# A two-layer encoder trunk: half of one tile's low-part products moved ahead of transposes, one product parted, and the mixer's products held to their written order

## The chip, the cores and the metric

One core of a Trainium2 chip runs the whole kernel. The metric is the device time of one execution in microseconds; three runs of the kernel before gave a median of 1097.06 us (1096.51 to 1097.66).

## What is computed

The reference is a two-layer encoder over 256 tokens of width 1024. Each layer has three sub-layers: a half-step SwiGLU feed-forward, a token mixer, and a second feed-forward. Each sub-layer starts with an RMS norm whose result is scaled and shifted by vectors that come from a conditioning input.

```python
for l in range(DEPTH):                      # 2
    n1 = modulate(rms_norm(h, norm_g[l, 0]), sh1, sc1)
    h = h + 0.5 * g1 * swiglu(n1, ffn_wg[l, 0], ffn_wu[l, 0], ffn_wd[l, 0])
    n2 = modulate(rms_norm(h, norm_g[l, 1]), sh2, sc2)
    y = token_mixing(n2, ...)    # 8-head grouped-query + 4-head differential attention, sigmoid gates, w_o
    h = h + g2 * y
    n3 = modulate(rms_norm(h, norm_g[l, 2]), sh3, sc3)
    h = h + 0.5 * g3 * swiglu(n3, ffn_wg[l, 1], ffn_wu[l, 1], ffn_wd[l, 1])
return rms_norm(h, final_g)
```

All data is float32. D_FF is 2816, so a feed-forward has 11 slices of 256 hidden columns.

## The kernel before

**Products.** TensorE (PE) works on float32r operands. Each operand is split into a high part and a low part (`whi`, `wlo` for a weight, `nh`, `nl` for the normed tokens), and a product is three matmuls: high by high, low by high, high by low (`mm3`, L85). Weights stream in from memory as units of 1 MB through four `raw` buffers. `pump` (L317) turns half a unit into `whi` (a copy on ScalarE, ACT, L328) and `wlo` (a subtraction on VectorE, DVE, L330). The same stream also carries conditioning units, which DVE reduces (L245) or adds into a gate row `gacc` (L276). `done` gives back the slots of a used half and pumps more. `load_next` issues the next load on SP's queue as soon as a unit has been used up.

**Boundaries.** Tokens stand in two tiles of 128. `boundary` (L444) ends a sub-layer and starts the norm of the next one. For tile 1 that is the residual (L441, L442), the sum of squares on ACT (L369), `rstd` on GpSimd (POOL, L124), the scaling `xs` on DVE (L394), eight transposes on PE (`transposes`, L403), then `nh` on ACT (`mod_hi`, L414) and `nl` on DVE (`mod_lo`, L426 and L429). `BT` (L35) holds for each kind of sub-layer how many halves of `mod_lo` of tile 0 are written early and how many `pump` calls stand before and after the end of tile 1's norm. The next sub-layer starts with the products of tile 0: `tok_hi` (L493) makes the 16 matmuls of 512 columns that need only `nh`, `tok_lo` (L505) the 8 that need `nl`. In a feed-forward these fill `gu`; in the mixer they fill `qa`, and the key and value projection `kv` follows. There are five boundaries: into the mixer of each layer, out of it, and from layer 0 to layer 1.

**Order.** The program is written as one list of instructions. A planner at compile time orders each engine's queue: of what its own timing says is ready it takes what is written first. The written order is therefore a priority, not the order of execution. `follow` (L90) adds an edge that forces one instruction behind another on the same engine. At run time each engine works through its queue in the planned order.

**The mixer around the change.** Its written order after the projections (L1026 to L1042) is: the query rows of tile 0 are transposed (`to_T` of `qr`), the key rows of tile 0 (`to_T` of `kr`), 48 products of the `qd` projection (`proj_T`, bank name `pt`), key rows of tile 1 are finished (`post_kv`), query rows and key rows of tile 1 are transposed, 48 more `qd` products, scores of tile 0 (`a_scores(0, 0)`, 12 matmuls), 48 `kd` products, scores of tile 1 (`a_scores(0, 1)`), 48 `kd` products, and the transposes `a_T(0, 0)` of the softmax rows of both tiles (bank name `pt` too, L875). Then come the 24 matmuls of the `vd` projection of tile 0, `a_T(0, 1)`, `a_scores(1, 0)` and the `vd` projection of tile 1. From there on, gate products (`gt`) stand between the attention steps.

A key row tile `kr` comes from this chain: squares on ACT, a reduction `hms` on DVE (L762), two small POOL steps (L763, L124), and a scaling on DVE (L825). A softmax row tile `p` comes from a maximum on DVE (`nmx`, L844), exponentials on ACT (L852), and a scaling (L864 on ACT for one key head, L866 on DVE for the other).

Of the kernel before, what the change touches and what calls it, by code (L numbers as in the profile page):

```python
# [34 lines left out]
BT = [(1, 1, 1), (1, 3, 1), (1, 1, 1)]  # L35
# [7 lines left out]
def trunk(tc, a):  # L43
    nc = tc.nc
    with (
# [38 lines left out]

        def mm3(out, Lh, Ll, Rh, Rl, start, stop):  # L85
            nc.tensor.matmul(out, Lh, Rh, start=start, stop=False, skip_group_check=True)  # L86
            nc.tensor.matmul(out, Ll, Rh, start=False, stop=False, skip_group_check=True)  # L87
            nc.tensor.matmul(out, Lh, Rl, start=False, stop=stop, skip_group_check=True)  # L88
# [26 lines left out]
        for hf in range(2):  # L115
            x = slice(hf * 512, (hf + 1) * 512)
            bank = gen("cb")
            cmm = nc.tensor.matmul(bank, ones[0:1, :], crow[hf], start=True, stop=True)
            cact = nc.scalar.activation(cb[:, x], bank, AF.Silu)
# [169 lines left out]
        def gate_bcast(l, s):  # L289
# [5 lines left out]
            for hf in range(2):  # L295
# [5 lines left out]
                nc.tensor.matmul(bank, onesr, gh, start=True, stop=False, skip_group_check=True)  # L301
                nc.tensor.matmul(bank, onesr, gl, start=False, stop=True, skip_group_check=True)
# [57 lines left out]
        class Norm:  # L360
# [37 lines left out]
            def transposes(self):  # L398
                self.banks = []
                for hf in range(2):  # L400
                    bank = gen("nt")
                    for i in range(4):
                        nc.tensor.transpose(bank[:, i * P:(i + 1) * P], self.xs[hf][:, i * P:(i + 1) * P], ident)  # L403
# [89 lines left out]
        def tok_hi(bank, ncol, unit_of, nT, t):  # L493
# [4 lines left out]
            for k in range(NK):  # L498
# [3 lines left out]
                nc.tensor.matmul(bank, nh[:, k, tok], wh[:, x], start=k == 0, stop=False, skip_group_check=True)  # L502
                nc.tensor.matmul(bank, nh[:, k, tok], wl[:, x], start=False, stop=False, skip_group_check=True)
# [45 lines left out]
        def first_T(hts):  # L549

            tb = gen("tb")
            for t in range(2):
                for c in range(2):
                    nc.tensor.transpose(tb[:, c * 256 + t * P:c * 256 + (t + 1) * P], hts[t][:, c * P:(c + 1) * P], ident)
# [6 lines left out]
        def ffn(i, nT, norm1, first, nT_next):  # L561
# [6 lines left out]
            def down_mm(idx, t, hf, last, y=slice(0, 512), part=False):  # L568
# [4 lines left out]
                for c in range(2):  # L573
                    x = slice(c * 512 + y.start, c * 512 + y.stop)
                    if part and c == 1:

                        for L, R in ((hh, wh), (hl, wh)):
                            nc.tensor.matmul(acc[t][hf], L[:, c, tok], R[:, x], start=False, stop=False, skip_group_check=True)
                        for z in (slice(0, PART), slice(PART, 512)):
                            nc.tensor.matmul(acc[t][hf][:, z], hh[:, c, tok], wl[:, 512 + z.start:512 + z.stop], start=False,  # L580
# [19 lines left out]
            else:  # L600
# [7 lines left out]
                tok_hi(banks[0], 512, uo, nT, 0)  # L608
                norm1.transposes()
# [107 lines left out]
        def mixer(i, nT, norm1, consts, nT_next):  # L717
# [65 lines left out]
            def to_T(src, dst, t, n):  # L783

                bank = gen("tt")
                for i in range(n):
                    nc.tensor.transpose(bank[:, i * P:(i + 1) * P], src[:, i * P:(i + 1) * P], ident)
# [44 lines left out]
            def a_scores(jj, t):  # L832
# [3 lines left out]
                for i in range(2):  # L836
                    for x, y in ((0, 0), (1, 0), (0, 1)):
                        for v in range(2):
                            pr = slice(v * 64, (v + 1) * 64)
                            nc.tensor.matmul(banks[v][:, i * 256:(i + 1) * 256], st["qaT"][x][pr, 2 * jj + i, tok], kaT[y][pr, 0, :],  # L840
# [29 lines left out]
            def a_T(jj, i):  # L870
                for v in range(2):
                    bank = gen("pt")
                    for t in range(2):
                        for c in range(2):
                            nc.tensor.transpose(bank[:, c * 256 + t * P:c * 256 + (t + 1) * P],  # L875
# [5 lines left out]
            def a_pv(jj):  # L881
                ot = gen("ot")

                for i in range(2):
                    for c in range(2):
                        for v in range(2):
                            nc.tensor.matmul(ot[v * 64:(v + 1) * 64, i * 256:(i + 1) * 256], va[:, c, v * 64:(v + 1) * 64],
# [12 lines left out]
            def b_scores(pair, t):  # L900
# [3 lines left out]
                for m in range(2):  # L904
                    ch = m * 2 + pair
                    for x, y in ((0, 0), (1, 0), (0, 1)):
                        for e in range(2):
                            pr = slice(e * 64, (e + 1) * 64)
                            nc.tensor.matmul(scs[e][:, m * 256:(m + 1) * 256], st["qdT"][x][pr, ch, tok], st["kdT"][y][pr, ch, :],
# [26 lines left out]
            def b_T(hd):  # L936
                bank = gen("wt")
                for t in range(2):
                    for c in range(2):
                        nc.tensor.transpose(bank[:, c * 256 + t * P:c * 256 + (t + 1) * P], xs[hd, t][0][:, c * P:(c + 1) * P], ident)  # L940
# [465 lines left out]
```

## Time and profile before

| what | value |
|---|---|
| median of three runs | 1097.06 us |
| the profiled execution, its own time | 1097.68 us |
| its span, first to last instruction | 1095.9 us |
| PE busy | 1082.9 us, 99% of the span |
| DVE busy | 864.9 us, 79% |
| ACT busy | 593.1 us, 54% |
| DMA | 271.12 MB, mean 247 GB/s |

Rows of a timeline give start and duration in us, the engine, the line, the operation, what it writes from what, its shape and a count; in brackets stands idle time ahead of it and what ended that. Durations of matmuls hold a modelled end, so spacing is read from one start to the next.

### The profile page before, as it was taken

How to read it: one execution, taken by the hardware profiler on the slowest of the kernel's cores; microseconds unless marked ns; L12 is line 12 of the kernel's file. 1: busy time of each engine (PE TensorE's matmuls, PEld its weight loads, DVE VectorE, ACT ScalarE, POOL GpSimd, SP SyncE). 2: the span in 40 equal slices, each digit the busy share in tenths (PEclk: the TensorE clock that was granted, in tenths of full speed). 3: DMA queues.
4: the chain of work that ended last, by engine and by line, in shares of the span. 5: the costliest groups of instructions: out<-in, count | busy, mean ns of one | idle time of the engine just before them, and what ended most of it. 6: DMA issues, size and time to landing. Idle time of an engine off the chain costs nothing.

```text
span 1095.9 us, 19235 instructions
## 1 busy us (share of the span) xinstructions
PE 1082.9 (99%) x7796; PEld 998.8 (91%) x7796; DVE 864.9 (79%) x1388; ACT 593.1 (54%) x916; POOL 44.5 (4%) x52
## 2 busy tenths in 40 slices
PE   8999999999999999999999999999999999999997
PEld 6989999898999899999989999989889998999996
DVE  5998986899978798886589886569988779766543
ACT  5564483558664554535455545435776547444432
POOL 1000000220010000000000000004000000000000
PEclk9999999999999999999999999999999999999999
DMA  8998996368745299997449987543865454876501
GB/s 315 380 368 336 380 335 219 120 263 332 264 172 193 86 376 357 347 377 266 150 152 357 365 288 285 202 165 126 297 236 189 157 190 183 315 267 229 197 19 39
DMA packets 44889, 271.12 MB, mean 247 GB/s; under 512 B 5880, under 2 KB 6648, under 8 KB 14848
## 3 DMA queue, kind: packets, MB, share of 16 engines
q1 hardware_dynamic: 42340, 267.93, 66.1%
q10 hardware_dynamic: 2460, 1.96, 0.6%
q8 instruction: 61, 1.00, 0.3%
q14 instruction: 28, 0.23, 0.1%
HBM read 268.82 MB, written 1.05 MB: 246 GB/s over the span
## 4 chain that ended last, share of the span: by engine, by line
PE 94%; DVE 3%; ACT 1%; issue 1%; POOL 0%; POOLq 0%
PE dn L87 6%; PE dn L88 6%; PE dn L86 6%; PE u L86 6%; PE g L86 6%; PE u L87 6%; PE g L88 6%; PE g L87 6%; PE u L88 6%; PE gt L86 3%; PE gt L88 3%; PE gt L87 3%; PE g L1199 2%; PE u L1199 2%; PE yb L88 1%; PE yb L87 1%
## 5 line engine op out<-in xcount | busy, mean ns | idle before, releaser
L330 DVE TENSOR_TENSOR wlo<-raw,whi 128x1024 fp32r<-128x1024 f32 x364 | 436.9, 1220 | 133.7 <-PE u L87 44.6
L328 ACT CAST whi<-raw 128x1024 fp32r<-128x1024 f32 x364 | 374.0, 1052 | 226.4 <-PE u L88 83.7
L86 PE MATMUL u<-nh,whi 128*128 128x256 f32 x592 | 164.0, 277 | 0.0
L86 PE MATMUL g<-nh,whi 128*128 128x256 f32 x592 | 164.0, 277 | 0.0
L87 PE MATMUL u<-nh,wlo 128*128 128x256 f32 x592 | 163.7, 277 | 0.0
L88 PE MATMUL g<-nl,whi 128*128 128x256 f32 x592 | 163.7, 277 | 0.0
L87 PE MATMUL g<-nh,wlo 128*128 128x256 f32 x592 | 163.7, 277 | 0.0
L88 PE MATMUL u<-nl,whi 128*128 128x256 f32 x592 | 163.6, 276 | 0.0
L86 PE MATMUL dn<-whi,hh 128*128 128x512 f32 (+1 forms) x326 | 126.0, 387 | 0.0
L87 PE MATMUL dn<-whi,hl 128*128 128x512 f32 (+1 forms) x326 | 125.9, 386 | 0.0
L88 PE MATMUL dn<-wlo,hh 128*128 128x512 f32 (+1 forms) x326 | 125.8, 386 | 0.0
L86 PEld LDWEIGHTS g<-nh,whi 128*128 128x128 f32 x592 | 111.2, 188 | 0.3
L87 PEld LDWEIGHTS g<-nh,wlo 128*128 128x128 f32 x592 | 111.2, 188 | 0.2
L86 PEld LDWEIGHTS u<-nh,whi 128*128 128x128 f32 x592 | 111.2, 188 | 0.1
L87 PEld LDWEIGHTS u<-nh,wlo 128*128 128x128 f32 x592 | 111.3, 188 | 0.0
L88 PEld LDWEIGHTS u<-nl,whi 128*128 128x128 f32 x592 | 111.2, 188 | 0.2
L88 PEld LDWEIGHTS g<-nl,whi 128*128 128x128 f32 x592 | 111.2, 188 | 0.0
L245 DVE CUSTOM_DVE_ANT_0 raw<-raw,cb 128x1024 f32<-128x1024 f32 x80 | 95.5, 1217 | 1.1 <-DMA raw<-in_ada_t_dram 0.9
L86 PE MATMUL gt<-nh,whi 128*128 128x256 f32 x256 | 73.7, 288 | 0.0
L88 PEld LDWEIGHTS dn<-wlo,hh 128*128 128x128 f32 x326 | 61.2, 188 | 12.4
L87 PEld LDWEIGHTS dn<-whi,hl 128*128 128x128 f32 x326 | 61.3, 188 | 11.1 <-DVE hl L546 0.2
L86 PEld LDWEIGHTS dn<-whi,hh 128*128 128x128 f32 x326 | 61.3, 188 | 11.1
(227 smaller groups left out, 2051.9 us busy)
## 6 DMA issues: line engine op xcount, KB each, us to landing
raw<-in_w_gu_dram SPq DMA_DIRECT2D x79, 1024.0 KB, 5.5
raw<-in_w_d_dram SPq DMA_DIRECT2D x41, 1024.0 KB, 6.4
raw<-in_ada_t_dram SPq DMA_DIRECT2D x40, 1024.0 KB, 6.8
raw<-in_ada_g_dram SPq DMA_DIRECT2D x24, 1024.0 KB, 6.3
raw<-in_w_in_dram SPq DMA_DIRECT2D x16, 1024.0 KB, 5.0
raw<-in_w_gate_dram SPq DMA_DIRECT2D x16, 1024.0 KB, 4.9
raw<-in_ada_t_dram SPq DMA_DIRECT2D x16, 512.0 KB, 6.5
raw<-in_w_gu_dram SPq DMA_DIRECT2D x32, 256.0 KB, 6.1
```

The costliest lines, as they stand in the source:

```text
L86: nc.tensor.matmul(out, Lh, Rh, start=start, stop=False, skip_group_check=True)
L87: nc.tensor.matmul(out, Ll, Rh, start=False, stop=False, skip_group_check=True)
L88: nc.tensor.matmul(out, Lh, Rl, start=False, stop=stop, skip_group_check=True)
L245: queue("dve", nc.vector.tensor_tensor_reduce(r, r, cb, 1.0, 0.0, op0=ALU.mult, op1=ALU.add, accum_out=col[:, k:k + 1]))
L328: split[1] = nc.scalar.copy(hi, r)
L330: split[0] = nc.vector.tensor_tensor(lo, r, hi.bitcast(F32), op=ALU.subtract)
L1199: nc.tensor.matmul(bank[:, c * 256:(c + 1) * 256], W[:, w], N[:, k, :], start=x + y + k + c == 0, stop=y == 1 and k == NK - 1, skip_group_ ...
```

## The change

It has four parts.

1. In a feed-forward (except the very first) and in the mixer, the first four of `tok_lo`'s eight products of tile 0 are written ahead of tile 1's transposes, and the other four stay behind them. Three of the pumps that stood in `tok_lo` are written in front of the second four.
2. The last product of `tok_lo` of tile 1 in a feed-forward is written as two matmuls of 264 and 248 columns.
3. At the boundary behind the first feed-forward of a layer, the `pump` that stood before tile 1's last products is written after tile 1's norm (`BT[0]`: one pump before and one after becomes none before and two after).
4. All PE instructions go through an object `pe`. Between `to_T` of the first query rows and the last gate product of the mixer, it forces each PE instruction behind the one written before it.

```diff
-BT = [(1, 1, 1), (1, 3, 1), (1, 1, 1)]
+BT = [(1, 0, 2), (1, 3, 1), (1, 1, 1)]
...
+        class Ordered:
+            on, last = False, None
+
+            def then(self, ins):
+                if self.on and self.last is not None:
+                    follow(ins, self.last)
+                self.last = ins
+                return ins
...
+        pe = Ordered()
...
-        def tok_lo(bank, ncol, unit_of, nT, t, last):
+        def tok_lo(bank, ncol, unit_of, nT, t, last, ks=range(NK), part=None):
...
-            for k in range(NK):
+            for k in ks:
                 u, i, c = unit_of(k)
                 wh, wl = half(u, i)
-                nc.tensor.matmul(bank, nl[:, k, tok], wh[:, c:c + ncol], start=False, stop=k == NK - 1, skip_group_check=True)
+                cut = [0, part, ncol] if part and k == NK - 1 else [0, ncol]
+                for z in range(len(cut) - 1):
+                    x = slice(cut[z], cut[z + 1])
+                    pe.matmul(bank[:, x], nl[:, k, tok], wh[:, c + x.start:c + x.stop], start=False, stop=k == NK - 1,
+                                     skip_group_check=True)
+                if ks.stop < NK:
+                    continue
...
                 tok_hi(banks[0], 512, uo, nT, 0)
+                tok_lo(banks[0], 512, uo, nT, 0, False, range(0, 4))
                 norm1.transposes()
                 norm1.mod_hi(l, s, nT)
                 norm1.mod_lo(l, s, nT)
                 behind.clear()
-                tok_lo(banks[0], 512, uo, nT, 0, False)
+                pump(3)
+                tok_lo(banks[0], 512, uo, nT, 0, False, range(4, NK))
                 tok_hi(banks[1], 512, uo, nT, 1)
-                tok_lo(banks[1], 512, uo, nT, 1, True)
+                tok_lo(banks[1], 512, uo, nT, 1, True, part=PART)
...
             tok_hi(qa[0], 512, uq, nT, 0)
+            tok_lo(qa[0], 512, uq, nT, 0, False, range(0, 4))
             norm1.transposes()
             norm1.mod_hi(l, 1, nT)
-            tok_lo(qa[0], 512, uq, nT, 0, False)
+            pump(3)
+            tok_lo(qa[0], 512, uq, nT, 0, False, range(4, NK))
...
             st["qaT"] = pair("qaT")
+            pe.on = True
             to_T(st["qr"][0], st["qaT"], 0, 4)
...
             gate_mm(7, 1)
+            pe.on = False
```

All other edits of the diff replace `nc.tensor.matmul` and `nc.tensor.transpose` by `pe.matmul` and `pe.transpose`.

## Rows read from the trace of the kernel before

**Rows 1.** The page's first part: busy time and share of the span.
```profile
PE 1082.9 (99%) x7796; PEld 998.8 (91%) x7796; DVE 864.9 (79%) x1388; ACT 593.1 (54%) x916; POOL 44.5 (4%) x52
```
**Rows 2.** Windows, layer 0's mixer: length, then busy time by engine, clock, DMA.
```profile
220.00:240.00 20.00, 20.00 (x176) 19.33 (x176) 19.37 (x37) 10.05 (x17) 7.21 (x8) 1.00 0.74 278
```
**Rows 3.** Timeline, boundary into layer 0's mixer: DVE, then PE.
```profile
202.78 1.27 DVE L276 SCALAR_TENSOR_TENSOR gacc<-raw,ccol,gacc 128x1024 f32<-128x1024 f32 x1
...
203.97 0.68 DVE L442 TENSOR_TENSOR h<-h,res 128x512 f32<-128x512 f32 x1
...
207.02 1.06 PE L403 MATMUL nt<-ident,xs 128*128 128x128 f32 x8 [0.97 <-DVE xs L394]
```
**Rows 4.** Timeline, boundary out of layer 0's mixer: PE and ACT.
```profile
373.29 0.40 PE L503 MATMUL gu<-wlo,nh 128*128 128x512 f32 x1
...
373.77 1.07 PE L403 MATMUL nt<-ident,xs 128*128 128x128 f32 x8
...
374.44 2.91 ACT L414 ACTIVATE nh<-nt,msh,ma 128x128 fp32r<-128x128 f32 x8 [1.27 <-PE nt L403]
```
**Rows 5.** Timeline, PE, a parted down product and the one behind it.
```profile
410.12 0.40 PE L580 MATMUL dn<-wlo,hh 128*128 128x264 f32 x2
410.35 0.40 PE L86 MATMUL dn<-whi,hh 128*128 128x512 f32 x1
```
**Rows 6.** Timeline, PE, layer 0's mixer: first qd product, first key transpose.
```profile
220.33 0.37 PE L86 MATMUL pt<-nh,whi 128*128 128x256 f32 x1
...
224.40 0.27 PE L787 MATMUL tt<-ident,kr 128*128 128x128 f32 x1
```
**Rows 7.** Timeline, DVE, layer 0's mixer: key rows of tiles 0 and 1.
```profile
223.71 0.42 DVE L825 TENSOR_SCALAR kr<-q,hr 128x64 f32<-128x64 f32 x2 [0.63 <-POOL hr L124]
...
232.21 0.41 DVE L825 TENSOR_SCALAR kr<-q,hr 128x64 f32<-128x64 f32 x2
```
**Rows 8.** Timeline, layer 1's mixer: first qd product, key rows of both tiles.
```profile
757.02 0.37 PE L86 MATMUL pt<-nh,whi 128*128 128x256 f32 x1
...
758.76 0.41 DVE L825 TENSOR_SCALAR kr<-q,hr 128x64 f32<-128x64 f32 x2
...
768.35 0.41 DVE L825 TENSOR_SCALAR kr<-q,hr 128x64 f32<-128x64 f32 x2
```
**Rows 9.** Timeline, PE, layer 1's mixer: starts of blocks from second kd half to a_pv.
```profile
776.83 0.38 PE L86 MATMUL pt<-nh,whi 128*128 128x256 f32 x1
...
782.38 0.60 PE L875 MATMUL pt<-ident,p 128*128 128x128 f32 x4
...
789.27 1.03 PE L875 MATMUL pt<-ident,p 128*128 128x128 f32 x8
790.23 0.97 PE L840 MATMUL sc<-kaT,qaT 64*128 64x256 f32 x12
791.13 0.50 PE L502 MATMUL pj<-whi,nh 128*128 128x512 f32 x1
...
796.83 0.44 PE L887 MATMUL ot<-pT,va 128*64 128x256 f32 x2
```
**Rows 10.** Timeline, layer 0's mixer: PE behind the scores, DVE's softmax steps, PE in vd.
```profile
240.39 0.38 PE L86 MATMUL pt<-nh,whi 128*128 128x256 f32 x1
...
244.76 0.67 DVE L844 TENSOR_REDUCE nmx<-sc 128x2 f32<-128x512 f32 x1
...
252.64 0.61 DVE L866 TENSOR_SCALAR p<-p,rs 128x256 f32<-128x256 f32 x2
...
256.23 0.50 PE L502 MATMUL pj<-whi,nh 128*128 128x512 f32 x1
```
**Rows 11.** Timeline, DVE, layer 1's mixer: softmax steps of tile 1.
```profile
780.31 0.67 DVE L844 TENSOR_REDUCE nmx<-sc 128x2 f32<-128x512 f32 x1
...
787.13 0.61 DVE L866 TENSOR_SCALAR p<-p,rs 128x256 f32<-128x256 f32 x2
```
**Rows 12.** Windows, the end of the span: PE's work and the mean granted clock.
```profile
1088.00:1096.00 8.00, 0.96 (x9) 0.76 (x7) 3.02 (x8) 1.95 (x5) 0.86 (x1) 0.87 0.17 66
```

More of the change, by code (lines that the diff above doesn't have):

```diff
@@ L83, in const, with matmul, transpose @@
             return sb.tile(list(shape), dt, tag=name, bufs=1, name=name)
+        class Ordered:
[5 more added lines that the diff above has]
+                return ins
+            def matmul(self, *args, **kw):
+                return self.then(nc.tensor.matmul(*args, **kw))
+            def transpose(self, *args, **kw):
+                return self.then(nc.tensor.transpose(*args, **kw))
+        pe = Ordered()
         def mm3(out, Lh, Ll, Rh, Rl, start, stop):
-            nc.tensor.matmul(out, Lh, Rh, start=start, stop=False, skip_group_check=True)
-            nc.tensor.matmul(out, Ll, Rh, start=False, stop=False, skip_group_check=True)
-            nc.tensor.matmul(out, Lh, Rl, start=False, stop=stop, skip_group_check=True)
+            pe.matmul(out, Lh, Rh, start=start, stop=False, skip_group_check=True)
+            pe.matmul(out, Ll, Rh, start=False, stop=False, skip_group_check=True)
+            pe.matmul(out, Lh, Rl, start=False, stop=stop, skip_group_check=True)
         def follow(ins, first):
@@ L117, in trunk @@
             bank = gen("cb")
-            cmm = nc.tensor.matmul(bank, ones[0:1, :], crow[hf], start=True, stop=True)
+            cmm = pe.matmul(bank, ones[0:1, :], crow[hf], start=True, stop=True)
             cact = nc.scalar.activation(cb[:, x], bank, AF.Silu)
@@ L300, in gate_bcast @@
                 nc.vector.tensor_tensor(gl, x, gh.bitcast(F32), op=ALU.subtract)
[L301 to L302 removed]
+                pe.matmul(bank, onesr, gh, start=True, stop=False, skip_group_check=True)
+                pe.matmul(bank, onesr, gl, start=False, stop=True, skip_group_check=True)
                 nc.scalar.mul(m["g"][:, hf * 512:(hf + 1) * 512], bank, 0.5)
@@ L402, in transposes @@
                     for i in range(4):
-                        nc.tensor.transpose(bank[:, i * P:(i + 1) * P], self.xs[hf][:, i * P:(i + 1) * P], ident)
+                        pe.transpose(bank[:, i * P:(i + 1) * P], self.xs[hf][:, i * P:(i + 1) * P], ident)
                     self.banks.append(bank)
@@ L553, in first_T @@
                 for c in range(2):
-                    nc.tensor.transpose(tb[:, c * 256 + t * P:c * 256 + (t + 1) * P], hts[t][:, c * P:(c + 1) * P], ident)
+                    pe.transpose(tb[:, c * 256 + t * P:c * 256 + (t + 1) * P], hts[t][:, c * P:(c + 1) * P], ident)
             tv = tb.rearrange("p (c x) -> p c x", c=2)
@@ L786, in to_T @@
                 for i in range(n):
-                    nc.tensor.transpose(bank[:, i * P:(i + 1) * P], src[:, i * P:(i + 1) * P], ident)
+                    pe.transpose(bank[:, i * P:(i + 1) * P], src[:, i * P:(i + 1) * P], ident)
                 tok = slice(t * P, (t + 1) * P)
@@ L874, in a_T @@
                         for c in range(2):
-                            nc.tensor.transpose(bank[:, c * 256 + t * P:c * 256 + (t + 1) * P],
+                            pe.transpose(bank[:, c * 256 + t * P:c * 256 + (t + 1) * P],
                                                 probs[jj, v, t][:, i * 256 + c * P:i * 256 + (c + 1) * P], ident)
@@ L939, in b_T @@
                     for c in range(2):
-                        nc.tensor.transpose(bank[:, c * 256 + t * P:c * 256 + (t + 1) * P], xs[hd, t][0][:, c * P:(c + 1) * P], ident)
+                        pe.transpose(bank[:, c * 256 + t * P:c * 256 + (t + 1) * P], xs[hd, t][0][:, c * P:(c + 1) * P], ident)
                 if hd % 2 == 0:
@@ L972, in b_outT @@
                 for hd in range(4):
-                    nc.tensor.transpose(bank[:, hd * P:(hd + 1) * P], on[:, hd * P:(hd + 1) * P], ident)
+                    pe.transpose(bank[:, hd * P:(hd + 1) * P], on[:, hd * P:(hd + 1) * P], ident)
                 if t == 0:
@@ L1263, in keep_busy @@
             for _ in range(n):
-                ins = nc.tensor.matmul(bank.rearrange("p (r x) -> p r x", r=4), ident, ident4, start=True, stop=True)
+                ins = pe.matmul(bank.rearrange("p (r x) -> p r x", r=4), ident, ident4, start=True, stop=True)
                 follow(ins, first_)
@@ L1289, in turn @@
             for i in range(4):
-                tr = nc.tensor.transpose(nts[t, hf][:, i * P:(i + 1) * P], xs[:, i * P:(i + 1) * P], ident)
+                tr = pe.transpose(nts[t, hf][:, i * P:(i + 1) * P], xs[:, i * P:(i + 1) * P], ident)
             return tr
```

18 lines of the change are left out of this document (9 added, 9 removed).

## The prediction

> **What bounds the kernel now.** I read the page's busy times first, then the windows, then PE's waits and its timeline at the five boundaries and through both mixers. PE is busy for 99% of the span [rows 1], so a change can gain only what PE still waits or wastes, while anything that makes PE wait is paid in full. In layer 0's mixer PE fills 20.00 of 20 us, and DVE 19.37 [rows 2]. DVE is nearly full there too, but it costs nothing as long as PE has something else to run. The reader is to see how PE keeps busy. The list has the key transposes of tile 0 ahead of the `qd` products; the queue runs 35 `qd` products first, from 220.33 to 224.40, and only then the key transpose [rows 6]. The planner filled a hole with products that were written later. At four of the boundaries PE is empty for about a quarter of a microsecond, at the fifth for about one.
>
> **Part 1 and 3, the boundaries.** At the boundary into layer 0's mixer PE sits idle 0.97 us for `xs` [rows 3]. Just before, DVE runs a gate addition of 1.27 us at 202.78, and the residual's second step starts only at 203.97, behind it. Part 3 writes one of these additions after the norm, so the norm may come 1.2 us sooner and PE may lose no time: a gain of up to 1.0. Four low-part products stand there ahead of the transposes already, by the planner's choice, so part 1 changes nothing. Bounds 0 and -1.0. At the boundary out of layer 0's mixer the last product starts at 373.29 and takes about 0.23 (24 such products take 5.70 [rows 9]); the transposes start at 373.77 [rows 4]. Part 1 fills that 0.25 us with four low products, 0.92 us, so that `xs` is ready when they are through. But behind the transposes there is then nothing but `tok_hi` of tile 1, which needs the first `nh`. ACT starts on it 0.67 us after the transposes, and eight activations take 2.91, so the first is there at 1.03 at the earliest. Eight transposes last 0.96 [rows 9] or somewhat less. So the 0.25 comes back as a hole of 0.1 to 0.3 behind the transposes. Sum 0, bounds -0.25 and +0.3; the two other boundaries into a feed-forward are alike, so -0.75 to +0.9 for three. Into layer 1's mixer the `kv` products cover that hole, and about 0.3 is gained. The pumps that move along feed DVE and ACT, and the one load that each used-up unit issues keeps its place in SP's sequence. PE waits for no weights at these places, so I take 0; uncovered, each pump would cost one 1.2 us subtraction.
>
> **Part 2.** Two matmuls of 264 and 248 columns take 0.23 us together where the kernel has them already [rows 5], as much as one of 512 takes. Four pairs: 0, at most +0.1.
>
> **Part 4, layer 0.** PE now takes the written order, so a transpose whose source is late holds up every product behind it, and the planner can no longer fill in. I walk PE along the list, first with DVE where it was. Prices [rows 9]: 48 products 5.55 us (776.83 to 782.38), eight transposes 0.96, twelve scores 0.90, the 24 `vd` products 5.70. PE is at the first `qd` product at 220.33 [rows 6]; the key rows are ready at 223.71 + 0.42 = 224.13 [rows 7], so it starts at 224.25, a wait of 3.9. DVE's chain sets that, so an earlier arrival through part 3 only lengthens the wait, and the 1.0 above is lost again. Then 48 products to 229.8 and four query transposes (0.35) to 230.15. The key rows of tile 1 are ready at 232.62 [rows 7]: PE goes on at 232.7, a wait of 2.5. Then 48, twelve scores, 48, twelve scores: 245.6, against 240.39 before [rows 10]; 48 more: 251.1. Next stand the softmax transposes. DVE took the first maximum of tile 1 at 244.76, 1.1 us before the new end of the scores; it can't run before 245.6, so the chain behind it moves by at least 0.85. Its last scaling ended at 253.25 and now ends at 254.1: a wait of about 3. From 254.3 on: `vd` 5.70, transposes 0.96, scores 0.90, two products 0.46: 262.3, where before PE had done the same work by 256.23. **+6.1.** (The waits sum to more, because before PE lost some 3 us in breaking up these blocks.)
>
> **Part 4, layer 1.** PE is there at 757.02, the keys at 759.17 and 768.76 [rows 8]. 759.25, 48 to 764.8, 0.35 to 765.15, wait 3.6 to 768.85, then 12.9 to 781.75 at the end of the second scores (before 776.83) and 787.3 at the softmax transposes. The maximum ran at 780.31 [rows 11] and now not before 781.8; the last scaling moves from 787.74 to 789.2, PE leaves the transposes at 789.3, and 5.70 + 0.96 + 0.90 later it is 796.85, against 791.13 [rows 9]. **+5.7.** Here too DVE's chain sets the time, and the 0.3 of part 1 is lost.
>
> **Bounds of part 4.** Below: the waits at tile 1's keys and at the softmax vanish, because DVE has worked off its queue while PE stood. Layer 0 then has 3.9 as its only wait and reaches the mark at 257.7 (+1.4), layer 1 at 792.1 (+1.0). Above: DVE stays as late behind the scores as it was, 253.25 - 240.39 = 12.9 us and 787.74 - 776.83 = 10.9: +10.4 and +9.1. I take the middle, because DVE's queue is the same work and what bounds it (DVE's own length) does not grow when PE stands.
>
> **Sum.** 1097.68 (the profiled execution's own time) + 6.1 + 5.7 + 0 = 1109.5; the median of the runs stands 0.6 below that execution: 1108.9. DVE may work off a little of its queue while PE stands, which pulls towards the lower bounds, so I say **1108**; this case's own range is 1104 to 1112.
>
> **Rivals.**
> *Only the first keys are waited for.* While PE stands 4 us, DVE finishes what is in its way, and the later chains meet PE in time: 1097.06 + 2.4 = 1099.5, with boundary holes up to 1104. For it: a wait of PE delays nothing of what DVE does next. Against it: DVE had 0.6 us of idle in these 20 [rows 2], so a stall of 4 us gives it only room for other pumped work.
>
> *The stalls grow.* DVE fills the stall with pumped work, and the softmax chain stays as late behind the scores as it was: 1097.06 + 19.5 = 1116.5. A lower clock would add to it. [...]
>
> *Faster.* The planner places the key chains earlier. `hms` of the keys stands behind pumped subtractions in DVE's queue; if the shifted pumps let it go four us sooner, the keys are ready when PE comes. It decides at keys ready by 220.4 and 230.2 in layer 0 and 757.0 and 765.2 in layer 1. Then the written order saves broken blocks: with no wait, the walks end 2.5 (layer 0) and 1.2 (layer 1) before the old marks, the boundaries into the mixers give 1.3 and the others 0.8: 1097.06 - 5.8 = 1091. Against it: nothing in the diff touches what is written ahead of the key chains except the place of a few pumps, and 2.2 to 3.9 us are missing.
>
> *It does nothing.* The planner's order already is the written one nearly everywhere from the first gate product on, so part 4 could bind nowhere. Rows 6 contradict it: the order differs there.
>
> **How the numbers follow.** The middle case 0.52, only the first keys 0.16, growing stalls or a lower clock 0.14, faster 0.15, nothing 0.03. The range runs from 1097 to 1117: it leaves out the faster case and the far end of the growing stalls, about 0.2. Within 0.2% (2.2 us, about what a measurement here can tell) lie the nothing case and a part of the first rival, 0.09; faster 0.15; slower 0.76.
>
> **What would show it.** In the profile after, PE should stand idle ahead of `tt<-kr` in both mixers, 2 to 5 us each, ended by DVE's `kr`, and ahead of `pt<-p`, ended by the scaling of `p`. PE's busy share should fall by about one percent, and the time from the first `nh` of a feed-forward to its end should not change. If PE shows no wait at the key transposes, the main step is wrong; if it waits there, but the span between mixers shrinks by several us, a gain was overlooked. If the granted clock is below 1.00 in a mixer, the second rival holds.

## The result, and the profile after

The changed kernel takes 1123.4 us (median of four runs, 1121.73 to 1123.72) against 1097.36 beside it: a ratio of 1.0234, with a 95% interval of 1.0216 to 1.0252. It is slower, as forecast, but by 26 us, where I said 11, and it lies above the range, which ended at 1117. Line numbers after the change are higher by 19 to 33 (PE's products are now all on L97, its transposes on L100). The page of the changed kernel, beside [rows 1]:

```profile
span 1121.4 us, 19244 instructions
PE 1088.3 (97%) x7799; PEld 1003.6 (89%) x7799; DVE 867.1 (77%) x1388; ACT 593.0 (53%) x916; POOL 45.5 (4%) x52
```

Every engine has nearly the work that it had; the time is PE's idle time and some slow products. These are PE's waits that are new (total, times, longest); only the third was there before, with 0.2:

```profile
PE tt L100 <- DVE kr L854: 9.8, 3, 3.6
PE tt L100 <- DVE msh L269: 3.4, 1, 3.4
PE pt L100 <- ACT p L893: 2.7, 2, 2.1
PE gu L97 <- DVE nl L448: 2.4, 3, 0.8
PE pt L100 <- DVE p L895: 1.9, 1, 1.9
```

These are 17.8 us in the mixers and 2.4 at the feed-forwards. The timeline has them where the prediction put them, with the tile 1 keys of layer 1 under another name (`msh` is a tiny step right behind `kr` on DVE):

```profile
223.47 0.47 PE L100 MATMUL tt<-ident,kr 128*128 128x128 f32 x1 [3.58 <-DVE kr L854]
...
235.59 0.30 PE L100 MATMUL tt<-ident,kr 128*128 128x128 f32 x1 [3.21 <-DVE kr L854]
...
258.33 0.87 PE L100 MATMUL pt<-ident,p 128*128 128x128 f32 x6 [2.10 <-ACT p L893]
...
773.22 0.33 PE L100 MATMUL tt<-ident,kr 128*128 128x128 f32 x1 [3.02 <-DVE kr L854]
...
782.90 0.45 PE L100 MATMUL tt<-ident,kr 128*128 128x128 f32 x1 [3.45 <-DVE msh L269]
```

Cutting the span at starts of the same PE rows in both traces gives the account (us, worked out from those starts; `ot` is the first product of attention times values):

| stretch | before | after | change | forecast |
|---|---|---|---|---|
| start to the first query transposes, layer 0 | 219.98 | 219.28 | -0.70 | 0 to -1.0 |
| first query transposes to `ot`, layer 0 | 41.49 | 52.85 | +11.36 | +6.1 |
| `ot` to the first query transposes, layer 1 | 495.19 | 497.47 | +2.28 | 0 |
| first query transposes to `ot`, layer 1 | 40.17 | 51.68 | +11.51 | +5.7 |
| `ot` of layer 1 to the end of the span | 299.07 | 300.12 | +1.05 | 0 |

In layer 0 the three waits sum to 8.9 us, less than the 9.4 of the forecast (3.9, 2.5 and 3). The profile counts a wait from the modelled end of the product before it, so these come out some 0.26 shorter than from row to row, as the forecast counted. Even so, most of the missing 5.3 us there is not longer waits. The windows show it (length, PE's busy time, then the other engines, granted clock, DMA):

```profile
219.00:223.40 4.40, 0.88 (x8) 0.64 (x7) 3.78 (x11) 2.30 (x4) 3.70 (x3) 0.89 1.02 389
223.40:229.40 6.00, 5.93 (x29) 5.94 (x30) 6.00 (x11) 2.42 (x4) 2.90 (x3) 0.51 0.48 176
229.40:232.20 2.80, 2.80 (x27) 2.73 (x25) 2.58 (x6) 0.00 (x0) 0.52 (x2) 1.00 0.71 231
235.50:239.50 4.00, 3.92 (x21) 3.95 (x22) 4.00 (x5) 1.21 (x2) 0.00 (x0) 0.57 0.48 160
773.20:778.90 5.70, 5.68 (x50) 5.68 (x51) 5.70 (x10) 1.68 (x4) 2.84 (x3) 1.00 0.60 220
782.80:785.70 2.90, 2.80 (x14) 2.83 (x15) 2.90 (x5) 0.27 (x1) 0.00 (x0) 0.52 0.95 359
806.50:811.00 4.50, 4.41 (x15) 3.65 (x16) 0.29 (x2) 0.58 (x1) 0.00 (x0) 0.67 0.57 224
```

Behind the wait of 3.58 us the granted clock is 0.51 for 6 us, with PE busy throughout: 29 instructions in 6.00 us, where it does 27 in the next 2.80 (four of them short transposes). Behind the second wait it is 0.57. In layer 1 it stays at 1.00 behind the first wait (3.02), and falls behind tile 1's keys (0.52) and behind the softmax (0.67). So it is low behind four of the six waits, and 1.00 behind 3.02 in layer 1 and 2.10 in layer 0 (1.00 from 258.30 to 264.00); the rows do not show what sets the two apart. Behind the wait of 3.58 some 0.21 us pass from one product to the next (starts at 223.95, 224.16 and 224.38), where 48 take 5.55 [rows 9], 0.12 each.

Along the prediction's walk, from the start of one step's first row to the start of the next one's, the changed kernel takes this much more than forecast (us):

| step | layer 0 | layer 1 |
|---|---|---|
| first query transposes to tile 0's keys | -0.1 | +1.0 |
| 48 products, up to tile 1's query transposes | +2.7 | +0.1 |
| from there to tile 1's keys | +0.9 | 0.0 |
| 48 products, up to the first scores | +1.8 | +1.6 |
| scores and `kd` products | 0.0 | +0.1 |
| softmax transposes, up to the first `vd` product | 0.0 | +1.9 |
| `vd` products and the rest, up to `ot` | -0.1 | +1.1 |

Of these 11 us, some 7.1 are products at the lower clock, 1.9 later keys and 1.9 a later softmax in layer 1.

### The profile page after: what moved, and what is told of

It reads as the page before. It is cut to its first block, busy times and chain, and to the rows that moved or that the text cites. A ratio compares the mean times of both kernels' runs of the same rounds, so it can differ in the third digit from the quotient of the medians.

```text
span 1121.4 us, 19244 instructions
## 1 busy us (share of the span) xinstructions
PE 1088.3 (97%) x7799; PEld 1003.6 (89%) x7799; DVE 867.1 (77%) x1388; ACT 593.0 (53%) x916; POOL 45.5 (4%) x52
## 3 DMA queue, kind: packets, MB, share of 16 engines
HBM read 268.82 MB, written 1.05 MB: 241 GB/s over the span
## 4 chain that ended last, share of the span: by engine, by line
PE 79%; DVE 11%; issue 4%; ACT 3%; DMA 2%; POOL 1%; POOLq 0%; SPq 0%; DVEq 0%; ACTq 0%
PE dn L97 21%; PE g L97 18%; PE u L97 18%; PE gt L97 5%; PE yb L97 4%; DVE wlo L349 3%; PE wo L97 3%; PE pt L97 2%; PE pj L97 2%; DMA raw<-in_w_gu_dram 2%; PE gu L97 2%; DVE raw L264 1%; DVE nf L445 1%; ACT whi L347 1%; DMA raw<-in_ada_t_dram 1%
## 5 line engine op out<-in xcount | busy, mean ns | idle before, releaser
L97 PE MATMUL g<-nh,whi 128*128 128x256 f32 x656 | 179.7, 278 | 1.3 <-ACT nh L1246 1.3
L97 PE MATMUL g<-nh,wlo 128*128 128x256 f32 x656 | 179.1, 277 | 0.1
L97 PE MATMUL u<-nh,whi 128*128 128x256 f32 x656 | 179.0, 277 | 0.0
L97 PE MATMUL u<-nh,wlo 128*128 128x256 f32 x656 | 178.9, 277 | 0.0
L97 PE MATMUL g<-nl,whi 128*128 128x256 f32 x656 | 178.8, 277 | 0.0
L97 PE MATMUL u<-nl,whi 128*128 128x256 f32 x656 | 178.7, 277 | 0.0
L97 PE MATMUL dn<-whi,hl 128*128 128x512 f32 (+1 forms) x358 | 138.5, 387 | 0.2 <-DVE hl L573 0.2
L97 PE MATMUL dn<-whi,hh 128*128 128x512 f32 (+1 forms) x358 | 138.5, 387 | 0.0
L97 PE MATMUL dn<-wlo,hh 128*128 128x512 f32 (+3 forms) x390 | 138.5, 369 | 0.0
L97 PEld LDWEIGHTS g<-nh,whi 128*128 128x128 f32 x656 | 123.2, 188 | 2.9 <-ACT nh L1246 1.9
L97 PEld LDWEIGHTS g<-nh,wlo 128*128 128x128 f32 x656 | 123.2, 188 | 0.7 <-DVE wlo L349 0.5
L97 PEld LDWEIGHTS u<-nl,whi 128*128 128x128 f32 x656 | 123.4, 188 | 0.0
L97 PEld LDWEIGHTS g<-nl,whi 128*128 128x128 f32 x656 | 123.4, 188 | 0.0
L97 PEld LDWEIGHTS u<-nh,wlo 128*128 128x128 f32 x656 | 123.3, 188 | 0.0
L97 PEld LDWEIGHTS u<-nh,whi 128*128 128x128 f32 x656 | 123.2, 188 | 0.0
L97 PEld LDWEIGHTS dn<-wlo,hh 128*128 128x128 f32 x390 | 73.3, 188 | 14.9
L97 PEld LDWEIGHTS dn<-whi,hl 128*128 128x128 f32 x358 | 67.3, 188 | 12.7 <-DVE hl L573 0.5
L97 PEld LDWEIGHTS dn<-whi,hh 128*128 128x128 f32 x358 | 67.3, 188 | 12.3
L97 PE MATMUL gt<-nh,whi 128*128 128x256 f32 x256 | 73.8, 288 | 0.0
```

Source lines behind the costliest of these rows:

```text
L97: return self.then(nc.tensor.matmul(*args, **kw))
```

## The experiments

**The parts apart.** Four runs undo or do parts. The first is the changed kernel less one line:

```
-            pe.on = True
```

> Parts 1 to 3 without the written order in the mixer. Theory (the order alone makes the key and softmax waits, and with them the lower clock; the boundaries cost about 0.9 us at three places and give about 1.2 at one): 1098.5 us, from 1097 to 1100, no wait ahead of the key transposes and a clock of 1.00 in both mixers. Rival (the moved pumps make the keys late, whatever the order): above 1105.

The second is the kernel before with part 4 alone, the third with `BT = [(1, 0, 2), (1, 3, 1), (1, 1, 1)]` alone, the fourth with part 1 alone (`tok_lo` cut in two around the transposes, `pump(3)` between).

> The kernel before with part 4 alone. Theory: nearly the whole loss, 1118 to 1123 us, with the granted clock near 0.5 behind the first key wait of layer 0. Rival (the parts only lose together): below 1110.

> The kernel before with part 3 alone. Theory: the gate addition leaves the way of the residual at the boundary into layer 0's mixer and PE's hole of 1 us there closes: 1096.0 us, from 1095.5 to 1096.7. Rival (something in the mixer takes it back): 1097.0 to 1097.8.

> The kernel before with part 1 alone. Theory (behind the transposes the second four products wait for the low halves, which stand behind a weight subtraction on VectorE): about 0.8 us lost at each of the three boundaries into a feed-forward, 1099.0 us, from 1098.3 to 1100.2, and in the trace a wait of the low products for the low halves. Rival (only the hole moves, as predicted): 1096.5 to 1097.6.

Measured: 1099.99 us without the written order (1.0022, 1.0013 to 1.0031); 1118.67 with it alone (1.0188, 1.0174 to 1.0202); 1097.07 with `BT` alone (0.9995, 0.9986 to 1.0004, no difference that can be told); 1100.61 with part 1 alone (1.0024, 1.0013 to 1.0035). So part 4 carries 21 of the 26 us and parts 1 to 3 some 2.4 (part 1 alone lies 0.4 above the range of its theory). The 2.6 that are left are no more than the intervals of the three kernels leave open together (2.7). The same cuts as above show where (change against before, us; the third column is the sum over the three boundaries into a feed-forward, from the transposes of tile 0's norm to those of tile 1's):

| kernel | tile 0's norm transposes to the first query transposes, layer 0 | layer 0's mixer | three feed-forward boundaries | layer 1's mixer |
|---|---|---|---|---|
| changed | -0.64 | +11.36 | +1.89 | +11.51 |
| without the written order | -0.63 | -1.01 | +1.92 | -0.23 |
| part 4 alone | +0.01 | +7.71 | -0.01 | +12.76 |
| part 1 alone | -0.08 | -0.12 | +1.94 | -0.05 |
| `BT` alone | -0.64 | -1.12 | +0.01 | +0.16 |

Part 1 costs some 0.64 at each such boundary: four products (0.92) for the hole of 0.25 that they fill, and it is not given back behind it. The low products that are left now meet a new wait. Before, PE has four low products and six of tile 1 between the transposes (373.77) and the second four; now it comes to these after two products of tile 1 and stands for `nl`. DVE has a pumped subtraction ahead of `nl` in both, and `nl` is done no later: 3.26 us behind the start of the transposes before, 2.60 now. Before, then after:

```profile
375.22 1.21 DVE L330 TENSOR_TENSOR wlo<-raw,whi 128x1024 fp32r<-128x1024 f32 x1
376.35 0.68 DVE L429 TENSOR_TENSOR nl<-nf,nh 128x512 fp32r<-128x512 f32 x1
...
377.09 1.19 PE L511 MATMUL gu<-whi,nl 128*128 128x512 f32 x4
...
385.75 1.04 PE L100 MATMUL nt<-ident,xs 128*128 128x128 f32 x8
...
386.54 1.21 DVE L349 TENSOR_TENSOR wlo<-raw,whi 128x1024 fp32r<-128x1024 f32 x1
387.67 0.68 DVE L448 TENSOR_TENSOR nl<-nf,nh 128x512 fp32r<-128x512 f32 x1
...
388.41 1.18 PE L97 MATMUL gu<-whi,nl 128*128 128x512 f32 x4 [0.77 <-DVE nl L448]
```

`BT` closes the hole at the first boundary and brings the mixer forward by 1.8 us up to `ot`, but 1.6 of these are lost between `ot` and the next boundary, 1.1 of them in a new wait:

```profile
PE wt L940 <- DVE xb L934: 1.1, 1, 1.1
```

**Low products behind the high ones.** Part 1 alone, with its second half moved:

```
-                tok_lo(banks[0], 512, uo, nT, 0, False, range(4, NK))
                 tok_hi(banks[1], 512, uo, nT, 1)
+                tok_lo(banks[0], 512, uo, nT, 0, False, range(4, NK))
```

> Part 1 alone, but in the feed-forwards the second four low-part products of tile 0 are written behind tile 1's products with the high part. Theory (part 1's loss at the three boundaries is the wait for the low halves, which the planner's timing sees as ready too early): that wait is gone, only a hole of 0.2 to 0.3 us behind the transposes is left, 1097.3 to 1098.6 us. Rival (the loss is the hole behind the transposes itself): 1100 to 1101, as with part 1 as it is.

1099.54 us (1.0019, 1.0009 to 1.0028). That lies between the ranges of the theory and its rival. The wait for `nl` is gone from the list of waits, and the first feed-forward is 0.67 shorter than before, but the two others are not (+0.07 and +0.59). So the wait is not all of the price, and what it is worth is not shown: the time cannot be told from that of part 1 as it is (1.0013 to 1.0035).

**Is it the clock?** Useless products of 512 columns fill PE's idle time ahead of the key transposes, in the changed kernel:

```
+            stay_busy(3)
             to_T(st["kr"][0], kaT, 0, 1)
...
+            stay_busy(3)
             to_T(st["kr"][1], kaT, 1, 1)
```

> The changed kernel with three useless transpose-sized products of 512 columns (some 0.9 us each) ahead of the key transposes of each tile in both mixers; nothing of the computation is left out. Theory (a part of the loss is the lower clock behind the waits, some 4.4 us in layer 0 and 2 to 3 in layer 1, and the later DVE steps that wait for PE's slow products): the clock stays at 1.00 in both mixers, 1114 to 1118 us. Rival (the waits alone set the time; what the clock takes, the softmax wait takes back): 1121 to 1125, clock 1.00 or not.

The second kernel has `stay_busy(5)` at tile 1's keys and `stay_busy(2)` ahead of `a_T(0, 0)`.

> As the run with three useless products ahead of the key transposes, but five ahead of tile 1's keys and two ahead of the first softmax transposes; nothing is left out. Theory (the lower clock costs some 7 us of the changed kernel's loss, and in the first warm run it still fell in layer 0 and at layer 1's softmax): clock 1.00 from the keys to the vd products in both mixers, 1115 to 1119 us. Rival (PE meets the same late sources whatever its clock): 1120 to 1123 with the clock at 1.00.

1120.77 and 1120.36 us, 2.6 and 3.0 less than the changed kernel, so about where the rival had them; the second's interval (1.0189 to 1.0223) still touches the changed kernel's. Its profiled execution was its slowest, 1122.89. In it, the clock stays up through layer 0's mixer (windows as above):

```profile
219.00:229.00 10.00, 8.83 (x62) 7.07 (x62) 9.38 (x19) 3.69 (x7) 6.66 (x6) 1.00 0.71 279
229.00:240.00 11.00, 10.61 (x65) 7.90 (x64) 10.96 (x18) 3.22 (x6) 0.95 (x2) 1.00 0.81 298
240.00:262.00 22.00, 21.62 (x160) 18.87 (x160) 18.71 (x40) 14.63 (x31) 0.00 (x0) 1.00 0.86 312
```

and that mixer still takes 50.39 us (219.27 to `ot` at 269.66), 8.9 more than before. (Behind layer 1's softmax the clock still fell, to 0.50 from 806.50 to 809.90.) PE comes to tile 1's query transposes at 229.22 instead of 231.77 and to the key transpose behind them at 229.66, but that starts only here:

```profile
234.50 0.30 PE L100 MATMUL tt<-ident,kr 128*128 128x128 f32 x1 [0.39 <-DVE kr L854]
```

PE now stands or runs useless products for 4.8 us at tile 1's keys, where I had 2.5. So the low clock was real, but it filled time that PE would have waited: of 4.5 us of stretched products in layer 0 only 2.5 come back.

**Does a later place for the transposes help?** In the changed kernel both key transposes are written behind all of `qd`, then the softmax transposes behind `vd0` too:

```
-            to_T(st["kr"][0], kaT, 0, 1)
...
-            to_T(st["kr"][1], kaT, 1, 1)
             proj_T("qd", 1, qd)
+            to_T(st["kr"][0], kaT, 0, 1)
+            to_T(st["kr"][1], kaT, 1, 1)
...
-            a_T(0, 0)                     (second kernel only)
             vd0 = proj("vd", 0)
+            a_T(0, 0)
```

> The changed kernel with both key transposes written behind the second half of the qd products. Theory (the key waits and the clock that falls in them are most of the loss): 1102 to 1110 us, no wait ahead of the key transposes, the softmax wait still there. Rival (DVE's own length bounds the mixer up to the softmax, so that PE only waits later): 1116 to 1121, with the softmax wait grown to 8 us or more.

> As the run with the keys later, and the first softmax transposes written behind the first vd products. Theory (what costs is late sources in the written order, not a fixed order as such): no wait is left in the mixers, the broken blocks of the planner's order are gone: 1095 to 1100 us. Rival (a fixed order costs in itself, by what the planner can no longer fill): above 1104.

1117.88 (1.0183, 1.0166 to 1.02) and 1111.64 us (1.0127, 1.0112 to 1.0142). Both miss what the leading theory expected; the first lies in its rival's range, but without the softmax wait of 8 us that the rival asked for (2.1 at most). The waits went one source further, in the first kernel to:

```profile
PE sc L97 <- DVE kaT L820: 4.7, 2, 3.8
PE tt L100 <- DVE qr L839: 4.2, 2, 2.4
PE pt L100 <- ACT p L893: 3.2, 2, 2.1
```

Moving two of the late sources leaves the others. So I wrote all of them late, in the kernel with part 4 alone: the projection is cut by `k`, and each transpose and score block stands behind products that cover its source.

```
 to_T qr0; qd 0-2; to_T kr0; qd 3; post_kv(1); qd 4-5; to_T qr1; qd 6-7; kd 0-1; to_T kr1; kd 2;
 a_scores(0, 0); kd 3; a_scores(0, 1); kd 4-7; vd0; a_T(0, 0); a_T(0, 1)
```

> Part 4 alone, but with the list of the mixer rewritten so that each transpose stands where its source is ready (keys of tile 0 behind 36 qd products, queries of tile 1 behind 72, keys of tile 1 behind 24 kd products, the first scores and the first softmax transposes later). Theory (what costs is a late source in a fixed order, and the clock that falls in the wait): no waits of PE above 1 us in the mixers, 1094 to 1099 us. Rival (a fixed order costs in itself): above 1104.

1099.88 us (1.0022, 1.0011 to 1.0033). That is 0.9 above the theory's range and far below the rival's. The order is still fixed, and 18.8 of 21 us are gone; one wait of 1.7 for the keys' low part is left in layer 0 and one of 1.0 for `p` in layer 1. A fixed order by itself costs little; it costs where it puts a late source ahead of products that could run. The same list with part 3 added:

> The same with part 3 too. Theory: 0.5 to 1.2 us less than the run before it, 1093 to 1098 us. Rival (what part 3 gives at the boundary is taken back at the keys): the same as that run within 0.3.

1102.79 us (1.0048, 1.0032 to 1.0064), 2.9 more, not less. The first query transposes come 1.2 sooner, and layer 0's mixer takes 3.80 instead of 1.46 more than before, with waits at the keys (1.40) and at the scores (2.62); layer 1's takes 1.83 instead of 0.55. PE comes 1.2 sooner, and tile 1's keys are scaled 1.8 later (234.38, 232.57 without part 3): DVE has six pumped operations between the two scalings there instead of four.

**Why are the sources late?** Part of it is in DVE's queue. These are the rows from tile 0's to tile 1's key scaling in the changed kernel (own steps left out):

```profile
222.99 0.42 DVE L854 TENSOR_SCALAR kr<-q,hr 128x64 f32<-128x64 f32 x2 [0.62 <-POOL hr L143]
...
225.78 1.27 DVE L295 SCALAR_TENSOR_TENSOR gacc<-raw,ccol,gacc 128x1024 f32<-128x1024 f32 x1
...
227.77 1.27 DVE L295 SCALAR_TENSOR_TENSOR gacc<-raw,ccol,gacc 128x1024 f32<-128x1024 f32 x1
228.97 2.35 DVE L349 TENSOR_TENSOR wlo<-raw,whi 128x1024 fp32r<-128x1024 f32 x2
231.24 0.28 DVE L791 TENSOR_REDUCE hms<-hsq 128x2 f32<-128x128 f32 x1
...
233.03 0.69 DVE L820 TENSOR_TENSOR qaT<-tt,qaT 128x512 fp32r<-128x512 f32 x1 [1.05 <-ACT qaT L819]
...
233.83 1.28 DVE L295 SCALAR_TENSOR_TENSOR gacc<-raw,ccol,gacc 128x1024 f32<-128x1024 f32 x1
235.03 0.41 DVE L854 TENSOR_SCALAR kr<-q,hr 128x64 f32<-128x64 f32 x2
```

Five pumped operations of 1.2 us stand between the two scalings; in the kernel before there are three (12.04 us from one to the other here, 8.50 in [rows 7]). And `qaT` of the queries, which needs PE's late transposes, stands ahead of the keys and holds DVE up for 1.05. With the clock kept up that hold is gone, and the two scalings are 10.89 apart: 2.4 more than before, two pumped operations. These two do not come from PE's standing still. With part 3 alone, in the planner's order and at no cost in time, DVE has the same five there:

```profile
222.41 0.42 DVE L825 TENSOR_SCALAR kr<-q,hr 128x64 f32<-128x64 f32 x2 [0.62 <-POOL hr L124]
...
225.19 1.28 DVE L276 SCALAR_TENSOR_TENSOR gacc<-raw,ccol,gacc 128x1024 f32<-128x1024 f32 x1
...
227.19 1.28 DVE L276 SCALAR_TENSOR_TENSOR gacc<-raw,ccol,gacc 128x1024 f32<-128x1024 f32 x1
228.38 2.36 DVE L330 TENSOR_TENSOR wlo<-raw,whi 128x1024 fp32r<-128x1024 f32 x2
...
232.10 1.29 DVE L276 SCALAR_TENSOR_TENSOR gacc<-raw,ccol,gacc 128x1024 f32<-128x1024 f32 x1
233.29 0.43 DVE L825 TENSOR_SCALAR kr<-q,hr 128x64 f32<-128x64 f32 x2
```

The scalings are 10.88 apart there, 8.50 with part 1 alone (three operations) and 9.10 with part 4 alone (four). So part 3 brings the two gate additions between the key chains, and the written order makes PE stand for the keys that they delay. In layer 1 nothing grows between the scalings (9.59 before, 9.60 after), but tile 0's keys are scaled 3.16 us behind PE's first query transposes instead of 2.10; it is 3.93 with part 3 alone and 2.01 with part 4 alone.

Three kernels write the chains ahead, with PE's written order unchanged:

```
+            post_kv(1, kv[1])
             proj_T("qd", 0, qd)
-            post_kv(1, kv[1])
...
+            post_kv(0, kv[0])             (second and third kernel)
             tok_mm(qa[1], 512, uq, nT, 1, True)
-            post_kv(0, kv[0])
...
+            a_norm(0, 0)                  (third; a_norm(0, 1) likewise)
             proj_T("kd", 0, kd)
-            a_norm(0, 0)
```

> The changed kernel, with only the chain that finishes tile 1's key rows written ahead of the first 48 qd products instead of behind them; PE's written order is the same. Theory A (the keys are late because DVE's own queue puts pumped work ahead of the chain: between the two key scalings the changed kernel has five pumped operations of 1.2 us in layer 0, the kernel before three): tile 1's key rows are there when PE asks, its waits of 3.2 and 3.4 us go, a part of them comes back at the softmax transposes: 1116 to 1120 us. Theory B (DVE is simply full in the mixer, whatever its order): pumped work only moves behind the chain and meets PE at the scores or the softmax: 1121 to 1124.

> As the run with tile 1's key chain written early, and tile 0's key chain is written ahead of tile 1's query products too. Theory A: without the five pumped subtractions (1.2 us each) that stand in and ahead of tile 0's key chain, its rows come some 3 us sooner, the first key wait falls from 3.6 and 3.0 to about 1, the clock does not fall there: 1108 to 1115. Theory B: 1118 to 1124, the waits stand elsewhere.

> As the run with both key chains written early, and the softmax scalings of each score block are written ahead of the kd products that follow it. PE's written order is still that of the changed kernel. Theory A: the softmax wait (2.1 and 2.6 us) shrinks as well: 1103 to 1111. Theory B: as in the two runs before, 1115 to 1124.

The fourth has the third's moves without the written order and without parts 1 to 3:

> The kernel before, with the key chains and the softmax scalings written early as in the run above, and with parts 1, 3 and 4 of the change left out, so that PE's order is again the planner's. In the kernel before PE has no wait in the mixers to remove, so both theories expect 1096 to 1099; a gain of more than 0.2% would say that the planner was still breaking up blocks because of late keys.

Two more leave the GpSimd steps of the key chain out, on the changed kernel and on the third of these:

```
+                if nheads == 2:
+                    return ms
                 nc.gpsimd.tensor_scalar(ms, ms, EPS, None, op0=ALU.add)
```

> The changed kernel without the two GpSimd steps in the key rows' chain (the added constant and the power of minus one half; the keys are scaled by the raw mean of squares instead, so that part of the computation is left out). Theory A' (the chain is long by its own steps: 3.4 us of GpSimd for tile 0's keys in layer 0, and DVE puts two subtractions of 1.2 us into that gap): the key rows come 1 to 3 us sooner, the first key waits of 3.6 and 3.0 us shrink to 1 to 2, the clock falls less: 1114 to 1119 us. Theory B (DVE is full in the mixers): the pumped subtractions stay ahead of the chain, 1120 to 1124.

> The kernel that writes both key chains and the softmax scalings first (1118.3 us, waits at the keys of 1.4 and 4.8 us in layer 0), without the same two GpSimd steps (the same part of the computation left out). Theory A': from the reduction to the key rows the chain then takes about 2 us instead of 4.3, and each key wait shrinks by 2 to 3 us: 1106 to 1113. Theory B: 1116 to 1120, since the waits move to the next late source.

Measured: 1118.4, 1124.08 and 1118.31 us for the three, 1097.91 without the order (1.0005, 0.9996 to 1.0015), 1122.5 and 1117.11 without the GpSimd steps. The first lies where theory A had it, and its waits at tile 1's keys did shrink (3.21 to 2.03, in layer 1 3.45 to 1.23). The second (0.08 above the range), the third and both kernels without GpSimd steps lie where the theory of a full DVE had them; without the written order there is no gain either. The third, with and without GpSimd steps, is 5 to 6 us faster than the changed kernel, which is clear of noise, but leaves 20 of the 26. PE's waits in layer 0's mixer, from the timelines:

| kernel | keys, tile 0 | keys, tile 1 | softmax | sum |
|---|---|---|---|---|
| changed | 3.58 | 3.21 | 2.10 | 8.9 |
| tile 1's key chain first | 3.48 | 2.03 | 2.86 | 8.4 |
| both key chains first | 1.21 | 4.79 | 2.95 | 9.0 |
| and the softmax scalings first | 1.39 | 4.80 | 2.18 | 8.4 |
| the same, no GpSimd steps for keys | 0.67 | 4.08 | 2.47 | 7.2 |
| changed, no GpSimd steps for keys | 2.94 | 3.31 | 2.10 | 8.4 |

The first wait can be had down to 0.67, and the others take it back. In the last kernel but one, tile 1's keys still make PE stand:

```profile
220.54 0.33 PE L100 MATMUL tt<-ident,kr 128*128 128x128 f32 x1 [0.67 <-DVE kr L856]
...
230.87 0.44 PE L100 MATMUL tt<-ident,kr 128*128 128x128 f32 x1 [4.08 <-DVE kr L856]
```

although DVE has no idle time between the two scalings there (220.08 and 230.31); it runs five pumped operations in these 10.2 us, as in the changed kernel. PE asks for tile 1's keys 6.2 us after tile 0's (220.54 to 226.79). A kernel without pumped work in the mixers was not tried, since those weights are what PE multiplies next; so that DVE's load, and not some other order of its queue, is the limit is argued from these six runs and [rows 2], and not shown.

## Why the prediction was right in sign and wrong in size

**Right.** Part 4 binds, against the rival that it does nothing. PE waits at the key transposes of both tiles and at the softmax transposes, in both layers; the first waits are 3.58 and 3.02 us (forecast 3.9 and 2.2). PE's share fell from 99% to 97%. The gain of part 3 at the first boundary is there (1.18 at the norm transposes of tile 1) and is lost again by the keys, as forecast. The time from tile 1's norm transposes to the next boundary changed by 0.26 and 0.07 us in the first two feed-forwards. The faster rival asked for keys that are ready when PE comes; they are not, and writing their chain first does not make them so.

**Wrong, the main term.** The step that failed is "I take the middle, because DVE's queue is the same work and what bounds it (DVE's own length) does not grow when PE stands." With part 4 alone the two mixers cost 20.5 us, where the middle has 11.8 and the upper bounds together 19.5. Two things were wrong in it: the sources came later than the walk has them (some 3.9 of the 11 us by rows), and PE's products ran at the lower clock (7.1, below). In layer 0 I kept tile 1's keys at 232.62, where they were. They come at 235.4 in the changed kernel, and at 234.4 even with the clock up. The queue up to them grew by two pumped operations, which part 3 moved there and which the forecast counted at nothing ("so I take 0"), and by a hold of 1.05 in which DVE waits for PE's own late transposes. In layer 1 tile 1's keys came as forecast, but tile 0's 1.0 later, and so did the softmax, 1.9 later: I had DVE take the first maximum right behind the second scores, which end at 797.42. It came 2.46 later, behind two pumped reductions:

```profile
797.46 1.21 DVE L264 CUSTOM_DVE_ANT_0 raw<-raw,cb 128x1024 f32<-128x1024 f32 x1
...
798.68 1.20 DVE L264 CUSTOM_DVE_ANT_0 raw<-raw,cb 128x1024 f32<-128x1024 f32 x1
...
799.88 0.67 DVE L873 TENSOR_REDUCE nmx<-sc 128x2 f32<-128x512 f32 x1
```

The last scaling ended 9.4 behind these scores instead of 7.4. In layer 0 it ended 8.7 behind them, 8.5 by the forecast; there "1.1 us before the new end of the scores" is a slip, since 245.6 less 244.76 is the 0.84 that the sum goes on with. With the clock up, PE is short of work for 3.9, 4.8 and 2.5 us at the three places of layer 0 (219.71 to 223.62, 229.66 to 234.50, 253.35 to 255.83), 11.2 where the forecast had 9.4, and the mixer grows by 8.9 instead of 6.1; 2.4 of these 2.8 lie at tile 1's keys.

**Wrong, the clock.** It stood in a rival at 0.14 and not in the sum. The granted clock fell behind both key waits of layer 0 (0.51 and 0.57) and behind tile 1's keys and the softmax of layer 1 (0.52 and 0.67), so by the sign that the prediction gave, the second rival holds in this. A block of 48 products takes 5.55 [rows 9]; at these clocks the two blocks in layer 0 took 2.7 and 1.8 more than that, and layer 1's stretches 1.6 and 1.1. Counted by rows that is the largest part of what the forecast missed. But it is not what the clock costs by itself: keeping the clock up gave back only 3 us of the whole, since the time went into the waits for late sources behind it (4.8 us at tile 1's keys in layer 0, where I had 2.5). The rival's other half, a softmax as late behind the scores as before (12.9 and 10.9), did not come: 8.7 and 9.4. Its 1116.5 is 7 us short.

**Wrong, the boundaries.** Zero, with bounds of -0.75 and +0.9 for three; measured +1.89, out of the bounds. Of the four products' 0.92 I had 0.25 filling the hole and the rest given back behind it. The rest comes back only if the products that stay behind are there to run, and they wait 0.77 for `nl`. I had looked at ACT's `nh` alone, not at DVE's `nl`, and not at how soon PE's queue would come to the second four products. The gain of 0.3 into layer 1's mixer is not there (23.06 us from tile 0's norm transposes to the first query transposes, 23.03 before). Part 2 was not run apart.

**Open.** Parts 1 to 3 and part 4 add up to 23.4 by themselves and cost 26.0 together, so a joint loss is not clear of noise. By the cuts, part 4 alone loses 7.71 and 12.76 in the two mixers and the changed kernel 11.36 and 11.51. In layer 0 the difference is at tile 1's keys: with part 4 alone PE goes on 0.71 us behind its query transposes, without a wait, and in the changed kernel 3.82 behind them. Why layer 1 loses less was not traced. There the kernel with the clock kept up took 52.59 us from the query transposes to `ot`, more than the changed kernel's 51.68; its useless products lie in that time, and I did not separate them.

## What to carry to other kernels

When a scheduler's order looks broken up, look at what its breaks cover before writing a tidy order over it: here they covered key rows that were 2 to 4 us late, and the tidy order paid for each of them. If an order is to be fixed, write each consumer behind enough independent products for its source (this brought 1118.7 down to 1099.9), and check all sources behind it as well, since a wait that is taken away lets the engine meet the next one sooner (with both key chains written first, the wait for tile 0's keys fell from 3.58 to 1.21 and that for tile 1's rose from 3.21 to 4.79). In a forecast, work the queues of the feeding engines out anew for every part of the change, rather than keep them where they were: a pump moved at a boundary put two operations of 1.2 us ahead of a key row 30 us later. And where PE is forecast to stand, price a lower clock in the sum: here it was 0.51 to 0.67 behind four of six waits, and the products there took some 7.1 us more.

## What the runs showed of the hardware

One GpSimd step of a key chain, a power of 128x2, took 0.73 to 3.18 us. In the changed kernel, tile 0's and tile 1's in layer 0:

```profile
219.84 3.12 POOL L143 TENSOR_TENSOR hr<-hms,mhalf 128x2 f32<-128x2 f32 x1
...
231.91 0.73 POOL L143 TENSOR_TENSOR hr<-hms,mhalf 128x2 f32<-128x2 f32 x1
```

Beside the long one DVE ran two weight subtractions (219.82 and 221.15, 1.22 each), beside the short one it stood for 1.05. With both key chains written first all four powers took 3.14 on average, against 1.93 in the changed kernel and 1.66 in the kernel before. So the chains that were moved up had longer powers; that they met DVE's pumped work there is argued from these rows, and spans on GpSimd are rough. Whether DVE's work makes the power longer was not shown: no run here took the two apart.

With three, five and two useless products in front of the three waits the clock was 1.00 in layer 0's mixer (0.51 and 0.57 behind the key waits without them), and the median was 3.0 us lower, of the 26 lost.
